# The causal mask times the inverse key norms, on VectorE instead of GpSimd, in a hybrid decoder layer

## The chip, the cores and the metric

The kernel runs on one core of one Trainium2 chip. The metric is the device time of an execution in microseconds (us), as a median of several runs. The engines are named as in the profile: PE (TensorE, the matmuls) with PEld (its weight loads), DVE (VectorE), ACT (ScalarE), POOL (GpSimd) and SP (SyncE, which here issues most DMAs).

## What is computed

One decoder layer on 2048 tokens of width 1024. RMSNorm, one wide projection, and three branches: A, an RWKV-7 recurrence with 8 heads of 64; B, a causal sliding-window attention of 128 tokens; C, a cross-attention into 256 memory tokens. Each branch is gated by a SiLU, projected, merged with sigmoid gates, and the sum goes through an output projection and is added to x. The change lies in branch A, of which this matters:

```
kk = heads(k * k_k)
kk = kk / jnp.maximum(jnp.linalg.norm(kk, axis=-1, keepdims=True), L2_EPS)
k = k * (1.0 + (a - 1.0) * k_a)
y = rwkv7_scan(rh, heads(decay), kh, vh, -kk, kk * ah)
# one step of the scan, state S per head:
sa = einsum('bhvk,bhk->bhv', S, a_t)
S = S * w_t[:, :, None, :] + sa[..., None] * b_t[:, :, None, :] + v_t[..., None] * k_t[:, :, None, :]
y = einsum('bhvk,bhk->bhv', S, r_t)
```

## The kernel before

The tokens are taken in four blocks of 512 (`TB`). In a block the recurrence works on chunks of 64 tokens (`C`; eight chunks, `NC_`) in chunked form: within a chunk, a triangular system is formed, inverted and applied, and from chunk to chunk a state is carried. The eight heads go in four pairs, p = 0 to 3; two pairs make a group. For each pair `rwkv_prep` (L671) builds the operands; for each group `rwkv_inverse` (L793) inverts the 32x32 triangular pieces on VectorE and `rwkv_chain` (L837) runs over the eight chunks. Beside this stream runs a second one, `stream_f` (L1255): cross-attention, sliding-window attention, their output projections, and the gates. Dense products are made of three passes in fp32r (`gemm3`, L457 to L459).

What `rwkv_prep` does around the change, in the order of the code:

- L716 to L721: sums of squares of the scaled key, per token and head, into `dk`, limited from below; L722: their reciprocal on VectorE. `dk` has one column for each chunk.
- L723, on GpSimd: the right half of the tile `AB` (128 partitions x 8 chunks x 128) is filled with the mask `gmask` (bf16); L724, also on GpSimd: the left half becomes the mask times `dk`, 128 x 512 elements. For the second pair of a group `AB` lies in a `whl` buffer, and so the profile names it `whl`. The other three tiles of a pair (QE, QO, BK) are named `whl` there too.
- L726 to L743, on VectorE and ScalarE: the scaled keys and receptances times decays, into `QE`, `QO` (L728, L742) and `BK` (L732, L737). L735 scales the key that L737 takes.
- L753: 16 matmuls for each pair (each in two records), `BK` against `QE` and `QO`, into PSUM tiles (rw, yps, oo).
- L760: VectorE multiplies those products by `AB`, in place, which is where the result of L724 is used. L761: VectorE multiplies them by the mask into `QE` and `QO`.
- L766: ScalarE copies pieces of `AB` for the inverse. L770: TensorE transposes `BK` into PSUM tiles rw, which must have been read by L760 and L761 first.

Other lines that are named below: L440 is VectorE's part of preparing a weight block (the low part of a hi/lo split; block 1 alone, since the split weights are kept in DRAM and reloaded later); L1060 splits the rotated queries of the sliding-window attention; L573 to L576 rotate them; L563 and L565 are the two sines of the rotary tables on ScalarE; L936 scales the softmax of the cross-attention, L999 transposes it; L677 is a one-element GpSimd memset that takes a buffer; L422 to L426 are GpSimd's powers for norms; L907 applies a norm to the recurrence's output.

The order of the work on each engine is not that of the code. `order` (L289) takes all instructions as recorded, and a list scheduler, `lay_out` (L181), fixes one order for each engine. It goes by costs written in the kernel, of which two bear on the change: for VectorE, `155 + 1.05 n + 30` ns for a two-input operation of n elements (L120), and for GpSimd 1300 ns for a two-input one with more than 256 elements (L128). Neither cost depends on what runs on the other engine. A change of one instruction's engine thus moves rows on every engine. On the chip each engine then executes its own order, and waits on semaphores for the others.

Of the kernel before, what the change touches and what calls it, by code (L numbers as in the profile page):

```python
# [14 lines left out]
ALU = mybir.AluOpType  # L15
# [12 lines left out]
C = 64  # L28
NC_ = TB // C
# [268 lines left out]
def build(tc, A, nsb=4):  # L298
    nc = tc.nc
    es = ExitStack()  # L300
    V, S, G, PE = nc.vector, nc.scalar, nc.gpsimd, nc.tensor
# [82 lines left out]
    gmask = cp.tile([128, 128], BF16, name="gmask")  # L384
# [279 lines left out]
    def tmp(tag="rt", bufs=NRT):  # L664
        return rp.tile([128, TB], F32, name=tag, bufs=bufs)
# [5 lines left out]
    def rwkv_prep(p, i, Z, dk, Nc, sb, hT, lwla, group):  # L671
        def big(name):

            if not i:
                return rp.tile([128, NC_, 128], F32, name=name)
            t = wp.tile([128, NC_, 128], F32, name="whl")
            G.memset(t[:, 0, 0:1], 0.0)  # L677
            return t

        QE, QO, AB, BK = (big(n) for n in ("QE", "QO", "AB", "BK"))  # L680
# [40 lines left out]
                    V.tensor_scalar(own[h, :, o], sums[at, :, e], 1e-24, None, op0=ALU.max)  # L721
        V.reciprocal(dk[:, i], dk[:, i])  # L722
        G.tensor_copy(AB[:, :, C:], gmask[:, C:].unsqueeze(1).to_broadcast([128, NC_, C]))  # L723
        G.tensor_tensor(AB[:, :, :C], gmask[:, :C].unsqueeze(1).to_broadcast([128, NC_, C]), dk[:, i].unsqueeze(2).to_broadcast([128, NC_, C]), op=ALU.mult)  # L724
        kkh = tmp()
        V.tensor_scalar(kkh, k, dcol("hk_k", p), None, op0=ALU.mult)  # L726
        for Q, h in ((QE, EV), (QO, OD)):
# [500 lines left out]
    for sb in range(nsb):  # L1228
# [12 lines left out]
        def stream_r():  # L1241
            n = 2
            for p0 in range(0, 4, n):
                group, Z = [], rp.tile([128, 2, 2, NC_, C], F32, name="Z")
                dk = xp.tile([128, 2, NC_], F32, name="dk", bufs=2)
                Nc = rp.tile([128, 2, NC_, 32], F32, name="Nc")
                for p in range(p0, p0 + n):
                    yield from rwkv_prep(p, p - p0, Z, dk, Nc, sb, hT, lwla, group)
                yield from rwkv_inverse(group, Z, Nc)
                yield from rwkv_chain(group, Z, dk, hT, yas)  # L1250
            while pend:
                pend.pop(0)()
            yield 0.412
# [125 lines left out]
```

## Time and profile before

| | us |
|---|---|
| median of 3 runs | 2248.6 (2247.82 to 2249.54) |
| the profiled execution | 2250.41 |
| its span | 2248.6 |
| PE busy | 2219.2 |
| DVE busy | 1531.7 |
| ACT busy | 926.1 |
| POOL busy | 149.7 |

Busy is the time in which an engine executes something; the span runs from the first to the last instruction. A group's row reads: line, engine, operation, output and inputs by name, shape, count, then busy us and the mean ns of one, then the idle time of that engine just before, and what ended it. A timeline's row reads: start, duration, engine, line, operation; in brackets the idle time before it and its releaser. A row of the waits reads: who <- whom, us in total, times, the longest. A row of the windows reads: the stretch, its length, then the busy time of PE, PEld, DVE, ACT and POOL (with the number of instructions), the granted clock, the DMA engines' share and GB/s.

### The profile page before, as it was taken

The page shows a single profiled execution, that of the slowest core. Times are in us where ns is not written, and L with a number is a line of the kernel's source. Part 1 is how long each engine was busy: PE and PEld are TensorE (multiplying, and loading weights), DVE is VectorE, ACT ScalarE, POOL GpSimd, SP SyncE. Part 2 cuts the span into 40 slices and gives each one's busy share as a digit, 9 for nine tenths or more (in the row PEclk, how much of TensorE's full clock was granted, in tenths as well). Part 3 has the DMA queues.
Part 4 walks back from the last instruction along what each step waited for, and adds up shares of the span by engine and source line. Part 5 has one row for each costly group of instructions (what it writes and reads, how often), then busy time and mean ns, then how long its engine had stood idle before and what let it go on. Part 6 is the DMA issues. An engine that isn't in the chain of part 4 may idle for free.

```text
span 2248.6 us, 36877 instructions
## 1 busy us (share of the span) xinstructions
PE 2219.2 (99%) x13706; PEld 1804.8 (80%) x13706; DVE 1531.7 (68%) x3951; ACT 926.1 (41%) x2024; POOL 149.7 (7%) x209
## 2 busy tenths in 40 slices
PE   8999999999999999999999999999999999999999
PEld 7887778778888778878888878787878887787887
DVE  6799699775479777953437957985245895896312
ACT  6664565545253354423214345442223435434210
POOL 2000010000000011000000001000000001100000
PEclk9999999999999999999999999999999999999999
DMA  6767556679944444447774434445675444343655
GB/s 215 271 232 245 191 188 220 221 269 353 324 146 160 134 141 150 147 165 235 239 239 136 164 122 150 148 135 195 229 250 199 157 142 160 115 148 132 206 191 193
DMA packets 146226, 430.55 MB, mean 191 GB/s; under 512 B 16640, under 2 KB 21120, under 8 KB 146048
## 3 DMA queue, kind: packets, MB, share of 16 engines
q1 hardware_dynamic: 129920, 398.83, 52.4%
q10 hardware_dynamic: 16128, 29.37, 4.0%
q8 instruction: 109, 1.79, 0.3%
q14 instruction: 69, 0.57, 0.1%
HBM read 333.24 MB, written 94.90 MB: 190 GB/s over the span
## 4 chain that ended last, share of the span: by engine, by line
PE 73%; DVE 18%; ACT 3%; DMA 2%; issue 2%; POOL 1%; SPq 0%; ACTq 0%; DVEq 0%; POOLq 0%
PE mm L457 18%; PE mm L459 18%; PE mm L458 17%; DVE ibc L803 2%; DVE ibc L804 1%; PE rw L881 1%; DVE Yi L805 1%; PE mm L1172 1%; PE mm L1173 1%; PE mm L1174 1%; ACT g L1102 1%; PE oo L1003 1%; DVE whl L440 1%; PE rw L866 1%; PE rw L874 1%
## 5 line engine op out<-in xcount | busy, mean ns | idle before, releaser
L457 PE MATMUL mm<-hH,whl 128*128 128x512 f32 x1888 | 750.0, 397 | 1.5 <-DVE gt L928 1.5
L459 PE MATMUL mm<-hH,whl 128*128 128x512 f32 x1888 | 748.3, 396 | 0.0
L458 PE MATMUL mm<-hL,whl 128*128 128x512 f32 x1888 | 748.0, 396 | 0.0
L457 PEld LDWEIGHTS mm<-hH,whl 128*128 128x128 f32 x1888 | 354.8, 188 | 72.7 <-DVE gt L928 1.9
L459 PEld LDWEIGHTS mm<-hH,whl 128*128 128x128 f32 x1888 | 354.8, 188 | 69.7
L458 PEld LDWEIGHTS mm<-hL,whl 128*128 128x128 f32 x1888 | 355.0, 188 | 67.8 <-issue 0.5
L439 ACT ACTIVATE whl<-raw 128x512 fp32r<-128x512 f32 x178 | 111.1, 629 | 144.8 <-PE mm L459 89.7
L440 DVE TENSOR_TENSOR whl<-raw,whl 128x512 fp32r<-128x512 f32 x178 | 123.3, 696 | 52.3 <-ACT whl L439 51.5
L457 PE MATMUL mm<-yh,whl 128*128 128x512 f32 x384 | 151.5, 395 | 1.4 <-DVE gt L1155 0.8
L459 PE MATMUL mm<-yh,whl 128*128 128x512 f32 x384 | 150.8, 393 | 0.0
L458 PE MATMUL mm<-yl,whl 128*128 128x512 f32 x384 | 150.7, 392 | 0.0
L872 ACT ACTIVATE SP<-Z,Pl 64x64 f32<-64x64 f32 x256 | 88.3, 345 | 112.7 <-DVE Z L882 109.2
L803 DVE STREAM_SHUFFLE ibc<-Nc 128x496 f32<-128x496 f32 (+30 forms) x248 | 113.3, 472 | 0.1
L1155 DVE SCALAR_TENSOR_TENSOR g<-g,mm 128x512 f32<-128x512 f32 x32 | 21.8, 680 | 128.6 <-PE mm L459 128.5
L804 DVE TENSOR_TENSOR ibc<-ibc,Yi 128x496 f32<-128x496 f32 (+30 forms) x248 | 104.4, 421 | 4.0
L805 DVE TENSOR_TENSOR Yi<-Yi,ibc 128x496 f32<-128x496 f32 (+30 forms) x248 | 102.9, 415 | 0.9
L1140 ACT ACTIVATE gt<-mm 128x512 f32<-128x512 f32 x64 | 38.0, 594 | 145.3 <-PE mm L459 145.1
L882 DVE SCALAR_TENSOR_TENSOR Z<-rw,Pl,SP 64x64 f32<-64x64 f32 x224 | 63.5, 283 | 50.0 <-PE rw L881 46.4
L457 PEld LDWEIGHTS mm<-yh,whl 128*128 128x128 f32 x384 | 72.1, 188 | 17.3 <-DVE g L1155 1.5
L459 PEld LDWEIGHTS mm<-yh,whl 128*128 128x128 f32 x384 | 72.1, 188 | 14.9
L458 PEld LDWEIGHTS mm<-yl,whl 128*128 128x128 f32 x384 | 72.1, 188 | 14.1
L1102 ACT ACTIVATE g<-g,mxs,st 128x256 f32<-128x256 f32 (+1 forms) x128 | 74.5, 584 | 18.8 <-DVE mxs L1095 18.6
(1812 smaller groups left out, 3786.7 us busy)
## 6 DMA issues: line engine op xcount, KB each, us to landing
whl<-k SPq DMA_DIRECT2D x486, 512.0 KB, 3.4
k<-whl SPq DMA_DIRECT2D x162, 512.0 KB, 4.3
raw<-in_w_in SPq DMA_DIRECT2D x118, 256.0 KB, 3.3
g<-in_x ACTq DMA_DIRECT2D x32, 256.0 KB, 4.4
out<-g ACTq DMA_DIRECT2D x32, 256.0 KB, 4.9
raw<-in_w_proj SPq DMA_DIRECT2D x24, 256.0 KB, 3.1
rt<-in_x ACTq DMA_DIRECT2D x24, 256.0 KB, 5.2
rt<-in_xt ACTq DMA_DIRECT2D x24, 256.0 KB, 5.8
```

What stands on the lines that cost most here:

```text
L439: S.activation(w[:, 0], raw, AF.Copy)
L440: V.tensor_tensor(w[:, 1], raw, w[:, 0].bitcast(F32), op=ALU.subtract)
L457: PE.matmul(out, lh, rh, start=i == 0, stop=False)
L458: PE.matmul(out, lh, rl, start=False, stop=False)
L459: PE.matmul(out, ll, rh, start=False, stop=i == n - 1)
L803: V.stream_shuffle(bc[:, :, :w], N_[:, :, s + 1:], [s] * 32)
L804: V.tensor_tensor(bc[:, :, :w], bc[:, :, :w], Y[:, :, s:s + 1].to_broadcast([128, n, w]), op=ALU.mult)
L805: V.tensor_tensor(Y[:, :, s + 1:], Y[:, :, s + 1:], bc[:, :, :w], op=ALU.add)
L872: S.activation(SP[h, i], Z[h, i, e, c], AF.Copy, scale=g[4][h, c:c + 1])
L882: upds = [V.scalar_tensor_tensor(Sst[h, g[0]] if c == NC_ - 1 else Z[h, i, e, c + 1], pS[h, i, e], g[4][h, c:c + 1], SP[h, i], op0=ALU.mul ...
L1102: S.activation(prs[b][:, i, m0:], prs[b][:, i, m0:], AF.Exp, scale=r2[:, b, i:i + 1], bias=mx[:, b, i:i + 1], accum_out=mx[:, b, 2 + i:3 + i])
L1140: S.activation(t, gp, AF.Tanh, scale=0.5)
```

## The change

One line: the multiply of L724 is issued on VectorE (`V`) and no longer on GpSimd (`G`). The operands are the same.

```
         V.reciprocal(dk[:, i], dk[:, i])
         G.tensor_copy(AB[:, :, C:], gmask[:, C:].unsqueeze(1).to_broadcast([128, NC_, C]))
-        G.tensor_tensor(AB[:, :, :C], gmask[:, :C].unsqueeze(1).to_broadcast([128, NC_, C]), dk[:, i].unsqueeze(2).to_broadcast([128, NC_, C]), op=ALU.mult)
+        V.tensor_tensor(AB[:, :, :C], gmask[:, :C].unsqueeze(1).to_broadcast([128, NC_, C]), dk[:, i].unsqueeze(2).to_broadcast([128, NC_, C]), op=ALU.mult)
         kkh = tmp()
```

What the scheduler makes of it is shown at three places. The first is VectorE in the second block, third pair (p = 2), from L735 to the first two L760. Before:

```order
L735 TENSOR_TENSOR rk__8671<-rk__8671,rt 128x512
L732 TENSOR_TENSOR BK<-rt 64x8x64
L742 TENSOR_TENSOR QE<-rr__8782,Pt 64x8x64
L732 TENSOR_TENSOR BK<-rt 64x8x64
L737 TENSOR_TENSOR BK<-rk__8671,rt 64x8x64 x2
L742 TENSOR_TENSOR QO<-rr__8782,Pt 64x8x64
L576 TENSOR_TENSOR g_8821<-g_8821,g_8823 128x512
L743 SCALAR_TENSOR_TENSOR rr__8782<-rr__8782,dv,rk__8671 128x512
L1060 TENSOR_TENSOR g_8828<-g_8821,g_8828 64x512
L1060 TENSOR_TENSOR g_8829<-g_8821,g_8829 64x512
L1152 SCALAR_TENSOR_TENSOR mB<-gt,mm 128x512
L760 TENSOR_TENSOR AB<-rw,AB 64x512 x2
```

The same place with the change:

```order
L735 TENSOR_TENSOR rk__8671<-rk__8671,rt 128x512
L724 TENSOR_TENSOR AB<-gmask,dk 128x8x64
L732 TENSOR_TENSOR BK<-rt 64x8x64
L742 TENSOR_TENSOR QE<-rr__8782,Pt 64x8x64
L732 TENSOR_TENSOR BK<-rt 64x8x64
L737 TENSOR_TENSOR BK<-rk__8671,rt 64x8x64 x2
L742 TENSOR_TENSOR QO<-rr__8782,Pt 64x8x64
L576 TENSOR_TENSOR g_8821<-g_8821,g_8823 128x512
L743 SCALAR_TENSOR_TENSOR rr__8782<-rr__8782,dv,rk__8671 128x512
L1060 TENSOR_TENSOR g_8828<-g_8821,g_8828 64x512
L1152 SCALAR_TENSOR_TENSOR mB<-gt,mm 128x512
L760 TENSOR_TENSOR AB<-rw,AB 64x512 x2
```

L724 has come in behind L735, and the second L1060 has moved behind the L760 and L761 that follow. Blocks 3 and 4 have the same rows. TensorE's rows from L753 to L770 are the same ones in both orders there.

The second place is VectorE in the first block, fourth pair (p = 3), from L722 on. Before:

```order
L722 RECIPROCAL dk<-dk 128x8
L732 TENSOR_TENSOR whl<-rt 64x8x64
L735 TENSOR_TENSOR rk__3604<-rk__3604,rt 128x512
L574 TENSOR_TENSOR g_3754<-g_3754,cosT 128x512
L440 TENSOR_TENSOR whl<-raw,whl 128x512
L737 TENSOR_TENSOR whl<-rk__3604,rt 64x8x64 x2
L1152 SCALAR_TENSOR_TENSOR mB<-gt,mm 128x512
L440 TENSOR_TENSOR whl<-raw,whl 128x512
L1073 COPY st_3831<-as__3830 128x8
```

With the change:

```order
L722 RECIPROCAL dk<-dk 128x8
L735 TENSOR_TENSOR rk__3604<-rk__3604,rt 128x512
L724 TENSOR_TENSOR whl<-gmask,dk 128x8x64
L737 TENSOR_TENSOR whl<-rk__3604,rt 64x8x64 x2
L440 TENSOR_TENSOR whl<-raw,whl 128x512
L743 SCALAR_TENSOR_TENSOR rr__3705<-rr__3705,dv,rk__3604 128x512
L574 TENSOR_TENSOR g_3754<-g_3754,cosT 128x512
L1152 SCALAR_TENSOR_TENSOR mB<-gt,mm 128x512
L1073 COPY st_3831<-as__3830 128x8
```

L574 and one L440 have moved from ahead of L737 to behind it, L732 stands ahead of L722 now, and L724 is there. Before the next L760, one L575 and one L440 follow in the new order, and L743 alone in the old one.

The third place is ScalarE in the first block, around the sines of the rotary tables. Before:

```order
L563 ACT_TABLE_LOAD
L563 ACTIVATE rt<-rt 128x512
L565 ACTIVATE rt<-rt 128x512
L439 ACTIVATE whl<-raw 128x512
L985 ACT_TABLE_LOAD
```

With the change:

```order
L927 ACTIVATE gt<-mm 128x512
L565 ACT_TABLE_LOAD
L565 ACTIVATE rt<-rt 128x512
L936 ACTIVATE g_1920<-g_1920,dn 128x256 x2
L936 ACTIVATE g_1923<-g_1923,dn 128x256 x2
```

The second sine (L565) has moved from behind the first one to a place after the exponentials of L985, with a table load of its own ahead of it; a further load follows before L1140. The order has 13 table loads, where it had 11.

More of the change, by code (lines that the diff above doesn't have):

```diff
@@ L723, in rwkv_prep @@
         G.tensor_copy(AB[:, :, C:], gmask[:, C:].unsqueeze(1).to_broadcast([128, NC_, C]))
-        G.tensor_tensor(AB[:, :, :C], gmask[:, :C].unsqueeze(1).to_broadcast([128, NC_, C]), dk[:, i].unsqueeze(2).to_broadcast([128, NC_, C]), op=ALU.mult)
+        V.tensor_tensor(AB[:, :, :C], gmask[:, :C].unsqueeze(1).to_broadcast([128, NC_, C]), dk[:, i].unsqueeze(2).to_broadcast([128, NC_, C]), op=ALU.mult)
         kkh = tmp()
```

## The prediction

> **What bounds the kernel now.** I read the page first: the span, the busy shares, the slices and the chain.
>
> ```profile
> span 2248.6 us, 36877 instructions
> ...
> PE 2219.2 (99%) x13706; PEld 1804.8 (80%) x13706; DVE 1531.7 (68%) x3951; ACT 926.1 (41%) x2024; POOL 149.7 (7%) x209
> ...
> PE   8999999999999999999999999999999999999999
> ...
> DVE  6799699775479777953437957985245895896312
> ...
> PEclk9999999999999999999999999999999999999999
> ...
> PE 73%; DVE 18%; ACT 3%; DMA 2%; issue 2%; POOL 1%; SPq 0%; ACTq 0%; DVEq 0%; POOLq 0%
> ```
>
> TensorE is busy for 2219.2 of 2248.6 us, at full clock. Only 29.4 us are left to be won by anything that is not less TensorE work, and this change takes no matmul away. GpSimd is busy for 7% and has 1% of the chain. The second view, busy time in four stretches, says where the 29.4 us lie.
>
> ```profile
> core 0: us, PE busy (x) PEld busy (x) DVE busy (x) ACT busy (x) POOL busy (x), PEclk, DMA share, GB/s
> 0.00:560.00 560.00, 543.75 (x3430) 442.75 (x3431) 449.73 (x1112) 317.84 (x674) 49.95 (x74) 0.99 0.69 240
> 560.00:1120.00 560.00, 556.92 (x3421) 452.87 (x3420) 379.39 (x979) 215.79 (x473) 34.26 (x47) 1.00 0.55 184
> 1120.00:1680.00 560.00, 556.94 (x3420) 452.54 (x3419) 360.44 (x948) 203.61 (x453) 34.27 (x47) 1.00 0.53 177
> 1680.00:2248.60 568.60, 561.64 (x3439) 456.69 (x3438) 342.16 (x913) 188.88 (x424) 31.19 (x41) 1.00 0.50 165
> ```
>
> 16.3 us (560 - 543.75) are idle in the first stretch, where VectorE is busy for 80%; 3.1, 3.1 and 7.0 us in the others, the last with the tail. The third view, TensorE's own waits, names whom it waits for.
>
> ```profile
> PE rw L866 <- DVE Z L882: 2.3, 4, 1.4
> PE rw L770 <- DVE QE L761: 2.1, 3, 0.7
> PE rw L753 <- DVE whl L737: 1.8, 1, 1.8
> PE mm L457 <- DVE gt L928: 1.5, 1, 1.5
> PE rw L770 <- DVE whl L761: 1.3, 3, 0.5
> PE rw L881 <- DVE Z L878: 1.3, 4, 0.4
> ...
> PE rw L785 <- DVE carry L661: 1.0, 3, 0.4
> PE rw L753 <- DVE QO L742: 0.8, 1, 0.8
> ```
>
> These eight rows hold 12.1 us, all of them waits for VectorE, none for GpSimd. Four rows (6.0 us, eight waits) stand at L753 and L770, right behind the place where the changed multiply feeds in: L753 needs BK and Q, and L770 needs the PSUM tiles that L760 and L761 read. So the question is whether VectorE gets later or earlier there.
>
> **The change part by part.** *Removed:* 16 multiplies on GpSimd, one for each of four pairs in four blocks.
>
> ```profile
> L724 POOL TENSOR_TENSOR AB<-gmask,dk 128x512 f32<-128x512 bf16 x8 | 11.5, 1436 | 52.7 <-DVE dk L722 52.7
> L724 POOL TENSOR_TENSOR whl<-gmask,dk 128x512 f32<-128x512 bf16 x8 | 10.9, 1358 | 185.2 <-DVE dk L722 185.2
> ```
>
> 22.4 us of GpSimd time, 1.40 us each. No row of the waits has an engine waiting for one of them, so the time that GpSimd is freed of is worth nothing by itself. But while they run, VectorE is slowed. Here is one of them, on VectorE and then on GpSimd:
>
> ```profile
> 826.14 0.64 DVE L735 TENSOR_TENSOR rk__8671<-rk__8671,rt 128x512 f32<-128x512 f32 x1
> 826.69 1.53 DVE L732 TENSOR_TENSOR BK<-rt 64x512 f32<-64x512 f32 x1
> 828.15 0.68 DVE L742 TENSOR_TENSOR QE<-rr__8782,Pt 64x512 f32<-64x512 f32 x1
> 828.84 0.69 DVE L732 TENSOR_TENSOR BK<-rt 64x512 f32<-64x512 f32 x1
> ```
>
> ```profile
> 826.30 1.38 POOL L724 TENSOR_TENSOR AB<-gmask,dk 128x512 f32<-128x512 bf16 x1 [1.77 <-DVE dk L722]
> ```
>
> The same L732 takes 1.53 us beside the GpSimd multiply and 0.69 without it: 0.84 us lost. The first and the last of the 16, each with the row that gives the usual duration (min/median/max):
>
> ```profile
> 73.29 1.56 DVE L440 TENSOR_TENSOR whl<-raw,whl 128x512 fp32r<-128x512 f32 x1
> ...
> 1963.17 2.09 DVE L732 TENSOR_TENSOR whl<-rt 64x512 f32<-64x512 f32 x2
> ```
>
> ```profile
> L440 DVE TENSOR_TENSOR whl<-raw,whl x178: 649/685/1559, 10.2 to 588.8; 128x512 fp32r<-128x512 f32 x178
> ```
>
> ```profile
> L732 DVE TENSOR_TENSOR whl<-rt x16: 629/686/1445, 117.8 to 1963.8; 64x512 f32<-64x512 f32 x16
> ```
>
> 1.56 - 0.69 = 0.87 us at the first; 2.09 - 2 x 0.69 = 0.71 at the last. Worked out in this way over all 16 (instructions that run beside one, less the median of their form), VectorE loses 0.47 to 0.88 us each time, 10.8 us in all.
>
> *Added:* 16 multiplies of 128x512 on VectorE. No row of before has this one there. Its nearest rows are L907, which also has one operand spread over 64 elements, and, as the upper bound, the slowest operation over 128x512 that reads a bf16 mask:
>
> ```profile
> L907 DVE TENSOR_TENSOR rt<-rt,var x16: 679/692/695, 283.8 to 2100.4; 128x512 f32<-128x512 f32 x16
> ```
>
> ```profile
> L697 DVE TENSOR_TENSOR_SCAN rt<-smask,rt 128x512 f32<-128x512 bf16 x16 | 19.6, 1224 | 0.5
> ```
>
> I take 0.69 us: 16 x 0.69 = 11.0 us, at most 16 x 1.22 = 19.6. **Net on VectorE: 11.0 - 10.8 = +0.2 us**, between 0 and +9. VectorE pays for this multiply already, as a stall in a neighbour, and will pay the same in the open. That is the main term, and it is zero.
>
> The Trainium skill, "Perfetto Trace Analysis", Optimizing Scalar/DVE Operations, says that moving operations between VectorE and GpSimd might not help, since the two share an SBUF read port. The rows above agree, with 0.68 us on average. "SBUF — State Buffer", Who interferes with whom, goes further: the one that loses the shared ports stands still for the other's whole instruction. By that the refund would be up to the 22.4 us of GpSimd's rows and VectorE would gain 11.4; the rows show about half of each instruction's span, and I go by them.
>
> *Moved:* the kernel's planner lays out every engine's order anew, so all else follows from the order. What TensorE executes is the same; counted in its order, a small matmul follows a 512-column one 438 times before and 434 times now. A return costs some 0.1 us (the 0.48 us of the row at 334.11 below, against 0.39 elsewhere), so this is -0.4 us, which I leave out. Three places count.
>
> (a) Third pair of blocks 2, 3 and 4, where TensorE stands 0.70 us at L770:
>
> ```profile
> 836.34 0.40 PE L458 MATMUL mm<-hL,whl 128*128 128x512 f32 x1
> 837.43 0.63 PE L770 MATMUL rw<-c_ident,BK 128*128 128x128 f32 x4 [0.70 <-DVE QE L761]
> ```
>
> ```profile
> 836.60 0.69 DVE L761 TENSOR_TENSOR QE<-rw,gmask 64x512 f32<-64x512 f32 x1
> ```
>
> In the new order one L1060 (0.69 us) stands behind L761 and no longer ahead of it; L724 (+0.69) comes in and the contention (-0.84) goes. L761 ends 0.84 us earlier, TensorE's rows between L753 and L770 are the same, and the wait of 0.70 goes: 3 x 0.7 = **-2.1 us**. It is 0 if VectorE is late there for another reason.
>
> (b) Fourth pair of block 1, where L753 waits 1.77 us for L737:
>
> ```profile
> 334.11 0.48 PE L457 MATMUL mm<-hH,whl 128*128 128x512 f32 x1
> 336.35 1.16 PE L753 MATMUL rw<-whl 64*128 64x128 f32 x16 [1.77 <-DVE whl L737]
> ...
> 340.43 0.63 PE L770 MATMUL rw<-c_ident,whl 128*128 128x128 f32 x4
> ```
>
> ```profile
> 332.26 1.44 DVE L735 TENSOR_TENSOR rk__3604<-rk__3604,rt 128x512 f32<-128x512 f32 x1
> ```
>
> Two operations (L574, L440; 0.68 us each) that stood ahead of L737 now stand behind it, and the inflated L735 (1.44 us) goes back to 0.68; L724 (0.69) comes in ahead. L737 comes 0.68 + 0.68 + 0.76 - 0.69 = 1.4 us earlier and most of the wait goes. But the two moved ones and one L575 now stand between L737 and L760: seven operations instead of four delay L761 by 2.0 us. TensorE took 4.1 us from the start of L753 to L770 (336.35 to 340.43), without a wait there; in the new order ten 512-column matmuls stand between them instead of eight. What is saved at L753 can come back at L770: between -1.8 and +0.6. I take **0**.
>
> (c) ScalarE's table loads:
>
> ```profile
> L565 ACT ACT_TABLE_LOAD x1 | 1.3, 1283 | 0.0
> ```
>
> There are two more in block 1, 2.6 us of an engine that is idle for 242 of the first 560 us. One stands ahead of L936, behind which L999 waits on TensorE. Between 0 and +2.6; I take half, **+1.3**.
>
> GpSimd's own queue only gets shorter: the memsets of L677, the copies of L723 and the statistics of L422 and L426 no longer stand behind a wait for dk. On SP's queue the loads of positions, km and vm move by one to three rows, and no row of TensorE's waits names one of them: 0. If (a) to (c) lacked their cover, the price would be that of the second rival.
>
> **The sum**: 0 - 2.1 + 0 + 1.3 = -0.8 us. The profiled execution took 2250.4 us (its span of 2248.6 and 1.8 around it), 1.8 above the median of the three runs. 2250.4 - 0.8 = 2249.6 there, and for the median 2248.6 - 0.8 = **2247.8 us**.
>
> **The rivals.**
>
> *Faster: the refund is worth more than the price.* For it: all eight waits at L753 and L770 are for VectorE, which is near full in the slices of block 1, and the planner's costs know nothing of the contention, so the new plan is nearer to what happens. At the eight waiting places the lost 0.68 us would come back whole, with the new multiply in a gap: the 6.0 us of waits go, and 2248.6 - 6.0 = 2242.6. The same time comes out if VectorE had been held for the whole 1.40 us of each GpSimd instruction: 1.40 - 0.69 = 0.71 us at eight places, 5.7 us. Against it: the rows show 0.68 lost, not 1.40, and most of these waits have other causes beside it. Chance 0.2, of which 0.05 is for the second way; it is the result that the ports' rule on "SBUF — State Buffer" in the Trainium skill would give.
>
> *Slower: the multiply delays VectorE where it has no slack, and the refund falls elsewhere.* L724 now stands in VectorE's own queue between L722 and L760, and the L732, L737, L742 and L760 behind it feed L753 and L770. At the eight places where TensorE already waits there, 0.69 us more of VectorE is 0.69 us of TensorE: 8 x 0.69 = 5.5, so 2254.1. It decides from the point at which VectorE's slack ahead of L753 or L770 is under 0.69 us. Against it: in the old order the stalled neighbour stood in the same queue, mostly between the same L722 and L760. Place (b) is its best case. Chance 0.2.
>
> *The change does nothing that can be seen:* no engine waited for GpSimd's multiply and the refund equals the price: 2248.6. Its sign is my forecast's, and it is counted there.
>
> **How the numbers follow.** My forecast, with waits that shift by a few us, has 0.6; its own range is 2244.1 to 2253.1, which is within 0.2%, about what a measurement of this kernel can tell from no change. Faster has 0.2, slower 0.2. The range reaches into both: 2241.5 (the faster rival and 1 us) to 2255 (the slower one and 1 us). The upper bound of the multiply (+9 on VectorE) lies within the slower rival's share.
>
> **What would show it.** In the changed kernel's profile: L724 on VectorE at 0.69 us; no L732, L735, L737 or L440 at 1.4 us beside GpSimd; VectorE's busy time within some 3 us of 1531.7; TensorE's busy time within 3 us of 2219.2. At (a) no wait at L770 in the third pairs; at (b) a shorter wait at L753 and a new one at L770; at (c) 13 table loads instead of 11. Wrong would be: a multiply of over 1 us, a wait of TensorE for L724 or L760 in every block, or idle time of TensorE that differs from 29.4 by over 5 us.

## The result, and the profile after

| | before | with the change |
|---|---|---|
| median of 6 runs, us | 2248.36 (2247.77 to 2251.1) | 2239.71 (2237.98 to 2242.34) |
| ratio, 95% interval | | 0.9960 (0.9949 to 0.9972) |
| profiled execution, us (its span) | 2250.41 (2248.6) | 2239.49 (2237.7) |

The change brings 8.65 us, 0.4%. The forecast was 2247.8 with 0.2 for "faster by over 0.2%", and its range began at 2241.5: the time lies outside it, on the fast side. Of all executions behind this document two stand far off, one of e1 (9907.6 us) and one of the kernel before beside it (5602.7 us), and the ratios leave them out. The page of the changed kernel:

```profile
span 2237.7 us, 36880 instructions
...
PE 2212.5 (99%) x13706; PEld 1804.9 (81%) x13706; DVE 1530.1 (68%) x3967; ACT 929.8 (42%) x2026; POOL 130.5 (6%) x193
...
DVE  6799799775479778953437967985245895896312
...
PE 74%; DVE 18%; ACT 3%; DMA 2%; issue 2%; POOL 1%; SPq 0%; DVEq 0%; POOLq 0%; ACTq 0%
```

VectorE has 16 instructions more (3967 against 3951) and is busy 1.6 us less. TensorE has the same 13706, is busy 6.7 us less and idle 25.2 us in place of 29.4. Its matmuls are pipelined: a row of 0.39 us starts every 0.23 us, so a short wait can hide in the rows, and busy and idle must be read together.

The steps from the start of one matmul to the start of the next hide nothing. For them, call a matmul wide if it is one in fp32r (8366 of the 13706, 7822 of them with 512 columns), and small if not; the prediction's counts of 438 and 434 are by the same division. The steps from a wide matmul to a small one take 134.9 us in sum (142.8 before), those from a wide one to a wide one 1803.3 (1806.5), all others as before within 0.5. Nearly three quarters of the profiled 10.9 us lie where TensorE turns to a small matmul. (The profiled execution of before lies 2 us above the median of its kernel, so 10.9 is more than 8.65.) The 3.2 us between wide matmuls are no more than executions differ by: e1, e7 and e8 below, with TensorE's order of before or very nearly so, have 1802.5 to 1805.1 there, and 141.5 to 142.2 for the turn to a small one. By line, the steps from a wide matmul into L770 and L753 are 3.9 and 3.2 us shorter, those into L866 2.2, and those into L483, L910 and L1003 1.2 us longer each.

The gain is spread over the program. The same four stretches, after:

```profile
0.00:560.00 560.00, 544.18 (x3444) 444.43 (x3445) 452.77 (x1121) 322.33 (x679) 46.34 (x70) 0.99 0.70 242
560.00:1120.00 560.00, 558.64 (x3436) 455.82 (x3435) 375.87 (x978) 214.69 (x471) 29.11 (x43) 1.00 0.55 186
1120.00:1680.00 560.00, 556.97 (x3424) 453.57 (x3423) 360.72 (x953) 203.77 (x453) 29.06 (x43) 1.00 0.54 177
1680.00:2237.70 557.70, 552.75 (x3407) 451.06 (x3405) 340.76 (x916) 189.04 (x424) 25.98 (x37) 1.00 0.49 165
```

TensorE gets through 14, 15 and 4 matmuls more in the first three stretches (3444, 3436 and 3424 against 3430, 3421 and 3420). Taken between the last L1174 of one block and that of the next, the four blocks take 3.1, 2.1, 3.0 and 2.6 us less. TensorE's waits:

```profile
PE rw L483 <- DVE g L478: 3.5, 2, 2.9
PE mm L457 <- DVE gt L928: 2.6, 1, 2.6
...
PE rw L866 <- DVE Z L882: 1.5, 4, 0.6
PE rw L910 <- DVE rt L907: 1.4, 2, 0.8
...
PE rw L770 <- DVE whl L761: 0.5, 1, 0.5
```

Two rows of before to compare, of which L483's was the largest there:

```profile
PE rw L483 <- DVE g L478: 2.5, 2, 2.0
...
PE rw L910 <- DVE rt L907: 0.4, 1, 0.4
```

Of the eight waits at L753 and L770 (6.0 us) one of 0.5 us is left. About 1 us each came back at L457 behind L928 (1.5 before), at L910 and at L483.

### The profile page after: what moved, and what is told of

The parts are those of the page before. It is cut to its first block, busy times and chain, and to the rows that moved or that the text cites. A ratio compares the mean times of both kernels' runs of the same rounds, so it can differ in the third digit from the quotient of the medians.

```text
span 2237.7 us, 36880 instructions
## 1 busy us (share of the span) xinstructions
PE 2212.5 (99%) x13706; PEld 1804.9 (81%) x13706; DVE 1530.1 (68%) x3967; ACT 929.8 (42%) x2026; POOL 130.5 (6%) x193
## 4 chain that ended last, share of the span: by engine, by line
PE 74%; DVE 18%; ACT 3%; DMA 2%; issue 2%; POOL 1%; SPq 0%; DVEq 0%; POOLq 0%; ACTq 0%
PE mm L457 18%; PE mm L458 18%; PE mm L459 18%; DVE whl L440 1%; ACT g L1102 1%; PE mm L1172 1%; PE mm L1173 1%; PE mm L1174 1%; PE oo L1003 1%; PE rw L881 1%; PE oo L1128 1%; PE rw L866 1%; PE rw L874 1%; DVE ibc L803 1%; DVE g L1090 1%
## 5 line engine op out<-in xcount | busy, mean ns | idle before, releaser
L457 PE MATMUL mm<-hH,whl 128*128 128x512 f32 x1888 | 749.0, 397 | 2.6 <-DVE gt L928 2.6
L458 PE MATMUL mm<-hL,whl 128*128 128x512 f32 x1888 | 749.6, 397 | 0.0
L457 PEld LDWEIGHTS mm<-hH,whl 128*128 128x128 f32 x1888 | 354.9, 188 | 74.0 <-DVE gt L928 3.0
L458 PEld LDWEIGHTS mm<-hL,whl 128*128 128x128 f32 x1888 | 354.9, 188 | 68.7 <-issue 0.2
L440 DVE TENSOR_TENSOR whl<-raw,whl 128x512 fp32r<-128x512 f32 x178 | 121.8, 688 | 47.1 <-ACT whl L439 46.3
L457 PE MATMUL mm<-yh,whl 128*128 128x512 f32 x384 | 151.7, 395 | 0.9 <-DVE gt L1155 0.9
L458 PE MATMUL mm<-yl,whl 128*128 128x512 f32 x384 | 150.6, 392 | 0.0
L1140 ACT ACTIVATE gt<-mm 128x512 f32<-128x512 f32 x64 | 38.1, 595 | 148.9 <-PE mm L459 148.6
L457 PEld LDWEIGHTS mm<-yh,whl 128*128 128x128 f32 x384 | 72.1, 188 | 16.0 <-DVE gt L1155 1.4
L458 PEld LDWEIGHTS mm<-yl,whl 128*128 128x128 f32 x384 | 72.1, 188 | 14.3
```

Of the source, the lines that this page charges most:

```text
L440: V.tensor_tensor(w[:, 1], raw, w[:, 0].bitcast(F32), op=ALU.subtract)
L457: PE.matmul(out, lh, rh, start=i == 0, stop=False)
L458: PE.matmul(out, lh, rl, start=False, stop=False)
L1140: S.activation(t, gp, AF.Tanh, scale=0.5)
```

## The experiments

Each was timed beside runs of the kernel before on the same chip (medians 2248.2 to 2249.4), so ratios compare best. The last column is TensorE's waits at L753 and L770 in the profile. "Told" is what VectorE's plan holds around the stretch from L722 to L760, for each pair, beyond the cost table's times of the operations that stood there before. L724 on VectorE counts there with 0.64 us, the time for which the plan keeps the engine: the 0.72 of the cost formula less 0.085 (L121). L735, which is told more in several runs, stands in that stretch in 10 to 15 of the 16 pairs of those runs, and ahead of L722 in the others.

| | multiply on | told, us | us | ratio (95%) | waits |
|---|---|---|---|---|---|
| before | GpSimd | 0 | 2248.4 | 1 | 6.0 |
| the change | VectorE | 0.64 | 2239.7 | 0.9960 (0.9949 to 0.9972) | 0.5 |
| e1 | VectorE | 0 | 2245.7 | 0.9990 (0.9981 to 0.9999) | 5.3 |
| e2 | GpSimd | 0.64 | 2241.4 | 0.9967 (0.9955 to 0.9979) | 1.0 |
| e3 | VectorE, L723 slows it | 0.64 | 2247.1 | 0.9994 (0.9985 to 1.0003) | 4.0 |
| e4 | ScalarE | 0 | 2237.5 | 0.9950 (0.9938 to 0.9963) | 0.4 |
| e5 | GpSimd, 8 pieces | 0 | 2493.0 | 1.1091 (1.1076 to 1.1106) | 18.6 |
| e6 | GpSimd | 0.69 (L735) | 2242.2 | 0.9976 (0.9967 to 0.9986) | 3.2 |
| e7 | GpSimd | 0 | 2247.6 | 0.9996 (0.9987 to 1.0005) | 6.0 |
| e8 | GpSimd | two moves by hand | 2248.7 | 1.0004 (0.9995 to 1.0013) | 4.3 |
| e9 | VectorE | 1.33 (L724, L735) | 2236.6 | 0.9946 (0.9933 to 0.9958) | 0 |
| e10 | GpSimd | 0 (L907 +0.69) | 2251.3 | 1.0011 (1.0002 to 1.0020) | 3.7 |
| e11 | GpSimd | 0 (L697 +0.50) | 2246.1 | 0.9991 (0.9982 to 1.0000) | 5.1 |
| e12 | GpSimd | 1.38 (L735) | 2237.4 | 0.9948 (0.9935 to 0.9960) | 0.4 |
| e13 | VectorE | 2.02 (L724, L735) | 2235.4 | 0.9939 (0.9925 to 0.9952) | 0 |
| e14 | ScalarE | 0.69 (L735) | 2232.0 | 0.9926 (0.9914 to 0.9938) | 0.3 |
| e15 | VectorE | 0.69 | 2242.7 | 0.9971 (0.9959 to 0.9982) | 2.7 |
| e16 | GpSimd | 0.69 (L743) | 2240.1 | 0.9959 (0.9945 to 0.9972) | 1.9 |
| e17 | GpSimd | 0 (L782 +0.69) | 2247.1 | 0.9987 (0.9979 to 0.9996) | 5.5 |

**First question: the engine or the order?** The change does two things: it moves 16 multiplies, and it lays out all engines anew. e1 and e2 do one each. A step is costed as if it were on the one engine, and issued on the other at its planned time:

```
+    moved = [s for s in todo if s.ins.name in planned]   # the 16 L724
+    for s in moved:
+        s.eng, s.lat = "POOL", LAT["POOL"]               # e1; "DVE" in e2
+        s.cost_POOL()
+    orders = lay_out(tc, todo)
+    for s in moved:
+        orders["POOL"].remove(s)
+    orders["DVE"] = sorted(orders["DVE"] + moved, key=lambda s: s.end - s.dur)
```

e1: the multiply on VectorE, in the order of before.

> The multiply runs on VectorE, but every engine's order is laid out as if it were on GpSimd, so that the orders are those of before, with L724 put into VectorE's at its planned time. Theory 'order' (the new layout brings the gain, and VectorE only pays openly what it paid as a stall): 2247 to 2250 us, no gain, waits at L770 and L753 as before. Rival 'engine' (VectorE wins by the end of the contention itself): 2238 to 2242 us, as the change. A value near 2244 would say that both bring about half.

2245.7 us: 2.7 less than before, by the interval between 0.2 and 4.3, and between the two expectations, nearer to "order". Its waits are those of before, a little shorter:

```profile
PE rw L770 <- DVE QE L761: 2.0, 3, 0.7
...
PE rw L753 <- DVE whl L737: 1.6, 1, 1.6
...
PE rw L770 <- DVE whl L761: 0.9, 3, 0.3
PE rw L753 <- DVE QO L742: 0.8, 1, 0.8
```

All four are rows of before, with 5.3 us in place of 6.0. So the engine by itself is not the gain, or not most of it.

e2: the multiply stays on GpSimd, in the order of the changed kernel.

> The multiply stays on GpSimd, but the orders are laid out as if it were on VectorE, so that they are those of the change, with L724 put into GpSimd's queue at its planned time. Theory 'order': 2238 to 2242 us, as the change, with VectorE's neighbours of L724 still stretched by about 0.7 us. Rival 'engine': 2247 to 2250 us.

2241.4 us: 7.0 less than before, with VectorE still losing 8.5 us beside GpSimd's L724 (worked out as in the prediction). Its waits at L770:

```profile
PE rw L770 <- DVE whl L761: 0.8, 1, 0.8
```

The order alone brings most of the gain, as "order" had it; what the engine adds in the new order (2241.4 to 2239.7) is within the two intervals.

e3: the change, with the mask copy of L723 made a two-input GpSimd operation behind L722, so that VectorE is held up again as before. TensorE's, ScalarE's and SP's orders are those of the changed kernel; on VectorE L724 stands a few rows later in some pairs.

```
-        V.reciprocal(dk[:, i], dk[:, i])
-        G.tensor_copy(AB[:, :, C:], gmask[:, C:].unsqueeze(1).to_broadcast([128, NC_, C]))
+        inv = V.reciprocal(dk[:, i], dk[:, i])
+        right = gmask[:, C:].unsqueeze(1).to_broadcast([128, NC_, C]); behind(G.tensor_tensor(AB[:, :, C:], right, right, op=ALU.mult), inv, True)
```

Its right half of AB holds the mask times itself.

> The change, with the fill of the mask's right half (L723) turned into a two-input GpSimd multiply that waits for L722, as L724 did before: TensorE's and ScalarE's orders are those of the change, the contention is back, and VectorE has the multiply as well. Theory 'VectorE has no slack at these places': VectorE gets about 16 x 0.7 = 11 us slower, and 5 to 9 us of that reach TensorE: 2245 to 2249 us. Rival 'slack' (the new order leaves VectorE more than 0.7 us at these places): 2239 to 2242 us.

2247.1 us: 7.4 of the 8.65 us are given back. The page, and the waits at L770:

```profile
PE 2216.2 (99%) x13706; PEld 1803.2 (80%) x13706; DVE 1538.5 (69%) x3967; ACT 930.3 (41%) x2026; POOL 145.7 (6%) x193
```

```profile
PE rw L770 <- DVE whl L761: 2.7, 4, 1.3
```

VectorE is busy 8.4 us longer than in the changed kernel, half a microsecond on average at each of 16 places, and the kernel is 7.4 us longer. At these places VectorE's time is nearly TensorE's time. So a price and a refund that cancel in VectorE's busy time may not cancel in the kernel's time where they fall at different spots; that is a reading, and no run tests it alone.

e4: the multiply on ScalarE, as eight copies with a scale per partition, in a layout of its own.

```
-        G.tensor_tensor(AB[:, :, :C], ..., op=ALU.mult)
+        for c in range(NC_): S.activation(AB[:, c, :C], gmask[:, :C], AF.Copy, scale=dk[:, i, c:c + 1])
```

> The multiply as eight ScalarE copies of 128x64 with the inverse norms as scale, in the layout that the planner makes of it: neither VectorE's price nor the contention. Theory 'VectorE time at these places is what counts': VectorE's busy time falls by about 11 us against the change and the time to 2232 to 2238 us. Rival 'order' (the layout decides, and each layout has waits of its own): anywhere from 2238 to 2250 us with no relation to VectorE's busy time.

2237.5 us, the least of these four:

```profile
PE 2212.0 (99%) x13706; PEld 1804.4 (81%) x13706; DVE 1521.7 (68%) x3951; ACT 956.6 (43%) x2152; POOL 126.9 (6%) x193
```

VectorE is 10.0 us less busy than before: that is the refund without the price. ScalarE pays 30 us for it and has them. But its layout is another one: a line-by-line comparison of TensorE's rows in the traces marks 3546 lines against the changed kernel, where the changed kernel has 1012 against before. Refund and layout are not told apart here.

**Second question: why is the new order better?** Theory "truth": the plan now reckons with about the 0.7 us that VectorE really spends at each of the 16 places, as a stall or in the open. Rival "luck": a new layout happens to be a good one. In e6 the multiply stays on GpSimd and L735 is told 0.69 us longer; in e7 L724 is told 0.30 us longer on GpSimd, where nothing hangs on it.

```
+    for s in todo:
+        if s.ins.name in planned:                        # e6: the 16 L735; e7: the 16 L724, 300
+            s.dur, s.busy = s.dur + 690, s.busy + 690
+    return lay_out(tc, todo)
```

> The multiply stays on GpSimd. The scheduler alone is told that each L735 takes VectorE 0.69 us longer than its cost table says (the time that VectorE loses beside GpSimd's multiply at each of the 16 places), and lays out all engines anew. Theory (truth in the plan): most of the 8.7 us came because the new order reckons with 0.69 us of VectorE between L722 and L760 that VectorE really spends there; then this gives 2240 to 2244, with the lost time beside GpSimd still at 8 to 11 us and with at most 1 us of waits left at L753 and L770. Rival (luck of a new layout): the order of the changed kernel happens to be a good one, and another new layout lands anywhere within some 4 us of 2248.4; waits at L753 and L770 of 2 us or more.

> The multiply stays on GpSimd; the scheduler is told 1600 ns for it instead of 1300, so that it lays out the orders anew without any more of VectorE's time in the plan. Theory (truth in the plan): nothing that bears on VectorE is changed, so 2247 to 2250, and the waits at L753 and L770 stay at 4 to 8 us. Rival (luck of a new layout): a shift of 3 us or more in either direction from so small a disturbance.

2242.2 and 2247.6 us, both as "truth" had it, save that e6 kept 3.2 us of waits at L753 and L770 where at most 1 was expected; 2 or more was the sign of "luck". e7 says nothing about "luck", since its layout is hardly new: TensorE's rows differ from those of before in 22 lines. e6 has GpSimd's multiply and a stretched VectorE (8.1 us beside L724), and an order that is not that of the changed kernel (1022 lines of difference on TensorE, counted as for e4): a second layout with nearly the same time told wins nearly the same.

e8: the two moves of the prediction, (a) and half of (b), made by hand in the order of before. On VectorE, in block 1 and in blocks 2 to 4:

```
 L735 TENSOR_TENSOR rk__3604<-rk__3604,rt 128x512
+L737 TENSOR_TENSOR whl<-rk__3604,rt 64x8x64 x2
 L574 TENSOR_TENSOR g_3754<-g_3754,cosT 128x512
 L440 TENSOR_TENSOR whl<-raw,whl 128x512
-L737 TENSOR_TENSOR whl<-rk__3604,rt 64x8x64 x2
...
-L1060 TENSOR_TENSOR g_8829<-g_8821,g_8829 64x512
 L1152 SCALAR_TENSOR_TENSOR mB<-gt,mm 128x512
 L760 TENSOR_TENSOR AB<-rw,AB 64x512 x2
...
 L761 TENSOR_TENSOR QO<-oo,gmask 64x512
+L1060 TENSOR_TENSOR g_8829<-g_8821,g_8829 64x512
 L509 TENSOR_TENSOR g_8885<-g_8819,g_8884 128x512
```

> The order of before on every engine, with GpSimd's multiply, and only two kinds of rows moved on VectorE: in the third pairs of blocks 2 to 4 the second L1060 behind the L761 that follow; in the fourth pair of block 1 the L574 and the L440 behind the two L737. Theory (each wait is late by what stands ahead of it on VectorE): the 0.70 us waits at L770 go in blocks 2, 3 and 4, and the 1.77 us wait at L753 falls by 1.37 us to 0.4, with no new wait in its place; 2.1 + 1.4 = 3.5 us, so 2244.9, block 1 shorter by 1.4 us and the others by 0.7 each. Rival (the waits come back elsewhere): within 1 us of 2248.4, the blocks within 0.4 us of before.

2248.7 us: nothing is won, as the rival had it. TensorE in block 2's third pair and in block 1's fourth:

```profile
835.51 0.63 PE L770 MATMUL rw<-c_ident,BK 128*128 128x128 f32 x4
...
840.20 0.50 PE L511 MATMUL as__8882<-g,ones 128*128 128x512 f32 x1 [0.87 <-DVE g L509]
```

```profile
333.42 1.16 PE L753 MATMUL rw<-whl 64*128 64x128 f32 x16 [0.67 <-DVE whl L737]
...
338.82 0.63 PE L770 MATMUL rw<-c_ident,whl 128*128 128x128 f32 x4 [1.30 <-DVE whl L761]
```

The 0.70 us at L770 are gone, and 0.87 us stand at L511 instead: the moved L1060 now delays L509, which feeds L511. In block 1 the wait at L753 fell by 1.1 us to 0.67, and 1.30 us came up at L770. Here a move past one wait only shifted it to the next consumer. The blocks of the profiled execution alone would have misled: block 1 is 1.1 us shorter than before and block 2 0.7, blocks 3 and 4, with the same move as block 2, not at all, and the medians show no gain.

e5: the multiply on GpSimd in eight one-input pieces (`for c in range(NC_): G.tensor_scalar(AB[:, c, :C], gmask[:, :C], dk[:, i, c:c + 1], None, op0=ALU.mult)`).

> The multiply stays on GpSimd, as eight operations of 128 x 64 with one input and a scalar per partition, in a layout of its own. If it is the second input that makes GpSimd hold up VectorE (L723, with one input, costs VectorE only 1.3 us in 16 executions), VectorE loses under 4 us in place of 10.8, its busy time is 1521 to 1526 us, and the time is 2240 to 2246. If GpSimd's operations hold VectorE up whatever their form, VectorE loses 8 us or more, its busy time is 1529 us or more, and the time is 2246 to 2252.

2493.0 us, far off both. What it says of VectorE holds: busy 1525.6 us, and the instructions beside these 128 pieces are no longer than their medians (0.05 us shorter in all). The time is lost elsewhere:

```profile
L724 POOL TENSOR_SCALAR AB<-gmask,dk x64: 435/750/1942, 72.0 to 2142.6; 128x64 f32<-128x64 bf16 x64
L724 POOL TENSOR_SCALAR whl<-gmask,dk x64: 435/750/1225, 136.1 to 2199.8; 128x64 f32<-128x64 bf16 x64
```

A piece takes 0.75 us in the middle, where the plan reckons with 0.23 (180 + 0.8 x 64 ns): a pair's eight take 6 us. TensorE is idle for 194 us at many lines (11.8 us at L770, 17.5 at L457 behind L1140), and returns to small matmuls 376 times in place of 438. TensorE is also busy 81 us longer than before, and its granted clock was 0.965 in this execution (0.998 before). Which of the wrong costs the layout broke on was not tried.

**Third question: truth, or room?** e9 tells the changed kernel 0.69 us more for L735 than is true. e10 and e11 tell the kernel before more at places outside the stretch from L722 to L760: 0.69 us too much at L907, and 0.50 us at L697, which is true (1.22 us in the profile). The edit is that of e6 on those lines.

> The changed kernel, and the scheduler is told 0.69 us too much for each L735, so that it reckons with 1.38 us of VectorE between L722 and L760 where VectorE spends 0.69. Theory (truth in the plan): the plan is now wrong again at these 16 places, on the careful side; the time is that of the changed kernel or longer, 2239 to 2244. Rival (more room ahead of L753 and L770 is what helps, true or not): another 2 us or more are won, 2234 to 2238. Rival (luck of a new layout): anywhere from 2238 to 2249.

> The kernel before, and the scheduler is told 0.69 us too much for each of the 16 L907, another operation of VectorE that occurs once per pair, far behind L770. VectorE loses nothing there on the chip (0.69 us each, as its cost table says), so that the plan gets further from what happens. Theory (truth in the plan): no gain, 2247 to 2251, with the waits at L753 and L770 at 4 us or more. Rival (any room in VectorE's plan helps): 2240 to 2244. Rival (luck of a new layout): 3 us or more either way.

> The kernel before, and the scheduler is told 0.50 us more for each of the 16 L697, the scan of the decays, which its cost table puts at about 0.72 us and which takes 1.22 us in the profile. Theory (truth in the plan): a true correction at another place of the pair's preparation, of about the same size (16 x 0.5 = 8 us of VectorE), brings something of the same kind: 2241 to 2246. If what counts is the stretch between L722 and L760 alone, L697 lies ahead of it and nothing is won: 2247 to 2250. Rival (luck of a new layout): anywhere within 4 us of 2248.4, and above it as likely as below.

e9 took 2236.6 us, where "truth" had 2239 to 2244: a plan made wrong on the careful side is no worse and probably better (the intervals of e9 and of the change overlap), with no wait left at L753 or L770:

```profile
PE rw L483 <- DVE g L478: 3.0, 2, 2.5
PE rw L881 <- DVE Z L878: 3.0, 5, 1.6
PE oo L362 <- ACT onesw L359: 2.4, 1, 2.4
PE mm L457 <- DVE carry L661: 1.8, 1, 1.8
```

e11, a true correction at another place, brings 0.09%, about 2 us, at the edge of nothing and between the two ranges expected of it. e10 loses 2.5 us, also at the edge of its interval, though its waits at L753 and L770 fell to 3.7. Others stand elsewhere (before, L457 had none behind L660, and L458 0.5):

```profile
PE mm L457 <- DVE rk__3604 L660: 2.7, 1, 2.7
...
PE mm L458 <- DVE mB L488: 1.2, 1, 1.2
```

From start to start, the turn to a small matmul fell by 9.0 us in e10 (142.8 to 133.8), and the steps between wide ones rose by 6.3 (1806.5 to 1812.8): waits at two lines are not the time. The loss itself is not in this profile, whose span (2247.9) is 0.7 us below that of before.

New theory, "room": what helps is more of VectorE's time in the plan between L722 and L760, spent or not. Three more kernels give it in other doses, e15 is a new layout with hardly more of it, and two ask where the room must stand.

> The kernel before, multiply on GpSimd, and the scheduler is told 1.38 us more for each L735 (about 0.68 us of it are really lost there beside GpSimd). Theory (room in the plan ahead of L753 and L770): as the changed kernel went from 2239.7 to 2236.6 with 0.69 us more, this goes from 2242.2 (0.69 us told) to 2237 to 2241. Rival (truth in the plan): 2242 or more. Rival (luck of a new layout): anywhere from 2240 to 2250.

> The changed kernel, and the scheduler is told 1.38 us too much for each L735. Theory (room in the plan): the room is used up at some point; with 0.69 us the waits at L753 and L770 were down to 2.4 us above the usual step, so at most 2 us more are won and the rest of the work is pushed behind: 2234 to 2239. Rival (truth in the plan): worse than with 0.69 us, 2239 or more. Rival (luck of a new layout): anywhere from 2236 to 2248.

> The multiply on ScalarE in eight pieces (2237.5 by itself), and the scheduler is told 0.69 us too much for each L735. Theory (room in the plan): another 1 to 3 us, 2234 to 2236.5, the fastest of all. Rival (truth in the plan): ScalarE's version already tells the plan all that happens, so 2237.5 or more. Rival (luck of a new layout): 2236 to 2247.

> The changed kernel, and the scheduler is told 0.05 us more for each L724, which shakes the layout as much as the change itself did (4541 lines of difference in TensorE's order) with next to no more room. Theory (room in the plan): 2238.5 to 2241, as the changed kernel. Rival (luck of a new layout): 3 us or more away from 2239.7, most likely back towards 2248.

e12 took 2237.4 us and e13 2235.4, both as "room" had it. "Truth" falls with e12: by it, 2242 or more was due, and the intervals of e6 and e12 lie apart. e14 took 2232.0, less than expected, and is the fastest of all: refund without price, and the room. e15 is the measure of luck: 0.05 us more told changes 1022 lines of TensorE's order in the traces, as many as the change itself did, and takes 2242.7, outside what "room" expected. Two layouts with nearly the same room thus lie 3 us apart, though their intervals overlap (0.9949 to 0.9972 and 0.9959 to 0.9982); the changed kernel may owe some of its 8.65 us to a good draw. e15 has the same order as e6 on TensorE, ScalarE and SP (0.64 + 0.05 is e6's 0.69), and so the pair asks the first question again: with the multiply on GpSimd 0.9976, on VectorE 0.9971, the same within the intervals.

> The kernel before, and the scheduler is told 0.69 us too much for each L743, which stands between L722 and L760 on VectorE but feeds neither L753 nor L770. Theory (room on the way to L753 and L770): L743 isn't on that way and can be put behind it, so little or nothing: 2246 to 2250. Variant (room anywhere between L722 and L760): as with L735, 2240 to 2244. Rival (luck of a new layout): anywhere within 4 us of 2248.7.

> The kernel before, and the scheduler is told 0.69 us too much for each of the 16 L782, behind L770. Theory (room on the way to L753 and L770): as with L907, nothing won, 2247 to 2252. Variant (any room in VectorE's plan of a pair): 2240 to 2244. Rival (luck of a new layout): anywhere within 4 us of 2248.7.

e16 took 2240.1 us: L743 feeds neither L753 nor L770, and room there is as good as at L735. So the variant is borne out, that it must stand in the stretch and not on the way itself; it is one run. e17, behind L770, brings 0.13%. The three places outside give 0.9987, 0.9991 and 1.0011; inside, every layout with 0.64 us or more lies at 0.9976 or below, but for e3, which spends the room. The three outside also change fewer of TensorE's lines (470 to 508), so they are a weaker test of luck.

Read by dose: on VectorE 2245.7, 2239.7, 2236.6, 2235.4 us with 0, 0.64, 1.33 and 2.02 told; on GpSimd 2248.4, 2242.2, 2237.4 with 0, 0.69 and 1.38; on ScalarE 2237.5 and 2232.0 with 0 and 0.69.

One reading puts e3 and e4 in line with the others: what is told, less what VectorE really spends there. It spends 0.68 us a pair where it executes L724, nothing where ScalarE does, and where GpSimd does the time that it loses (0.68 in the order of before, 0.47 to 0.69 in the others); in e3 the half microsecond beside L723 comes on top. Told 0.5 to 0.7 us too little (before, e1, e3, e7, e8, e10, e11, e17), the ratios are 0.9987 to 1.0011; told right within 0.2 us (the change, e2, e4, e6, e15, e16), 0.9950 to 0.9976; told 0.6 to 1.4 us too much (e9, e12, e13, e14), 0.9926 to 0.9948. Layout alone does not do this: e3 has TensorE's order of the change and falls into the first group. But the groups were read off afterwards, no run was made to test them, within a group the times still lie 5 to 6 us apart, and e5 is in none.

## Why the prediction was wrong

**The main term was right in VectorE's time.** L724 on VectorE:

```profile
L724 DVE TENSOR_TENSOR AB<-gmask,dk x8: 676/684/687, 72.7 to 1910.1; 128x512 f32<-128x512 bf16 x8
L724 DVE TENSOR_TENSOR whl<-gmask,dk x8: 676/683/686, 123.7 to 1954.1; 128x512 f32<-128x512 bf16 x8
```

0.68 us for 0.69, and VectorE's busy time went by -1.6 us where +0.2 was forecast. The kernel's time, at an equal order, went by -2.7 (e1), of which the interval leaves 0.2 to 4.3. The sentence that only TensorE's 29.4 idle us can be won was too narrow: 6.7 of the profiled 10.9 us came out of its busy time, which was to stay within 3 us of 2219.2.

**The step that failed is "Three places count", the worth of the new order.** It was read from two spots, and -2.1 + 0 + 1.3 us were put down; the order alone brings 7.0 (e2). Point by point:

(a) The wait at L770 in the third pairs went, as forecast:

```profile
832.73 0.63 PE L770 MATMUL rw<-c_ident,BK 128*128 128x128 f32 x4
...
837.42 0.50 PE L511 MATMUL as__8882<-g,ones 128*128 128x512 f32 x1 [0.19 <-DVE g L509]
```

But the reason given, one L1060 moved and the contention gone, does not hold as it stands. The end of the contention is not needed: in the new order with the contention still there (e2, the L732 at 1.53 us) the three waits go too, and without it in the order of before (e1) they stay, 2.0 us of 2.1. And the moved L1060 is not enough: in e8 the same move cost 0.87 us at L511. In the changed kernel L511 waits 0.19 us only, since it starts 4.69 us behind L770, as in e8, but with three matmuls more in between (18 rows against 15). The re-laid TensorE is part of (a), and the prediction looked at it only between L753 and L770.

(b) was taken as 0, "between -1.8 and +0.6", and this term was mis-sized. Here is the fourth pair of block 1, TensorE and VectorE:

```profile
332.96 1.16 PE L753 MATMUL rw<-whl 64*128 64x128 f32 x16
...
338.05 0.63 PE L770 MATMUL rw<-c_ident,whl 128*128 128x128 f32 x4 [0.54 <-DVE whl L761]
```

```profile
329.48 0.64 DVE L735 TENSOR_TENSOR rk__3604<-rk__3604,rt 128x512 f32<-128x512 f32 x1
330.03 0.69 DVE L724 TENSOR_TENSOR whl<-gmask,dk 128x512 f32<-128x512 bf16 x1
330.64 1.38 DVE L737 TENSOR_TENSOR whl<-rk__3604,rt 64x512 f32<-64x512 f32 x2
```

The 1.77 us went and 0.54 came back at L770: -1.2. The direction of the trade was seen, its balance was not. The refund has the smaller part in it, as e2 shows, where the contention still stretches L737's two to 2.11 us:

```profile
332.65 1.16 PE L753 MATMUL rw<-whl 64*128 64x128 f32 x16
...
338.04 0.63 PE L770 MATMUL rw<-c_ident,whl 128*128 128x128 f32 x4 [0.84 <-DVE whl L761]
```

The new order alone takes 1.77 away and brings 0.84, the moved multiply a further 0.3. In e8, with two of VectorE's rows moved and TensorE's order that of before, 1.1 went and 1.3 came back.

Not counted in the sum: the three 0.45 us waits at L770 in the fourth pairs of blocks 2 to 4 and the 0.8 us at L753 in block 1. They went too (no row after), 2.1 us.

(c) The 13 table loads came (L565 x2, L1140 x5) and 1.3 us were charged; behind L936 TensorE waits 0.4 us (0.6 before). It cost nothing that shows.

Together the waits at L753 and L770 hold 5.5 us less, and the steps into these two lines, with what hides in the busy rows, 7.1. Elsewhere gains (L866) and losses (L483, L910) nearly cancel. So the prediction looked at the right two lines: it had three of their eight waits right, took one as nothing on balance, left four out of its sum, and charged 1.3 us for the table loads. The rival "faster: the refund is worth more than the price", with 6.0 us of waits gone and 2242.6, was nearest, at 0.2. Its reason, a plan nearer to what happens, holds in part: a plan that is short of VectorE's time loses, but e9 and e13 are further from what happens on the other side and faster still. The rival "slower" failed on VectorE's slack: e3 shows that 0.5 us more at each of the 16 places costs 7.4 us, so such time is as dear as that rival said; but the refund came with the price, and the new plan holds the time for it.

**What stays open:** which of the planner's moves carry the gain (the waits at L753 and L770 fall with it in nearly all kernels, but not in e10), and what share of the changed kernel's 8.65 us is the draw of one layout. By e6, e15 and e16 a layout with 0.69 us told takes 2240 to 2243.

## What to carry to other kernels

Where a scheduler lays out the program by costs, moving an instruction also changes what the plan reckons with, and that can be worth more than the instruction: test it apart, by telling the plan the new cost and leaving the work where it is. A move past one wait has no known worth until the next consumer of the delayed operation has been looked at. And when an engine feeds a full one, its time in the plan ahead of the hand-over is worth padding: 0.69 us on top of a plan that was about right brought 3.1 (e9), 4.8 (e12) and 5.5 us (e14) here, the next 0.69 brought 1.2 (e13).

## What was not expected of the hardware

A two-input GpSimd multiply of 128x512 cost VectorE about as much (0.68 us in the mean in the order of before, 0.47 to 0.69 in others) as VectorE needs to do it itself (0.68 us). Eight one-input GpSimd pieces of 128x64 cost VectorE nothing that can be measured (e5), though they took GpSimd about 6 us for a pair. ScalarE's eight copies with a scale (e4) are short and even, 2.7 us for a pair, on an engine that is idle for over half of the span:

```profile
L724 ACT ACTIVATE AB<-gmask,dk x64: 330/334/354, 71.9 to 1909.2; 128x64 f32<-128x64 bf16 x64
L724 ACT ACTIVATE whl<-gmask,dk x64: 331/334/350, 122.7 to 1953.0; 128x64 f32<-128x64 bf16 x64
```
